# Weight-sum copies from SyncE between its loads, accumulations alone from GpSimd, and a sixth raw tile

## The chip, the core and the metric

The kernel runs on one core of a Trainium2 chip. Five engines work side by side, each in the order of its own instruction queue: TensorE (PE, matrix products, with its weight loads shown as PEld), VectorE (DVE), ScalarE (ACT), GpSimd (POOL) and SyncE (SP), which here only issues DMAs. GpSimd and ScalarE issue DMAs too. An engine that waits for a semaphore holds up everything behind it in its queue. The metric is the device time of one execution in microseconds (us); lower is better. The time before is the median of three runs, 763.82 us (761.96 to 764.92).

## What is computed

One layer of a streaming encoder on 512 frames of width 1024, all in float32:

```python
hn = rmsnorm(h, norm_mix_g[l])
proj = hn @ w_in[l]
fq, fk, fv, ff, gq, gf, gi, gg = jnp.split(proj, split_idx, axis=-1)
fox_out = fox_attention(...)         # 8 heads of 64, causal, with a forget bias F[t] - F[s]
rec = hgrn2_chunkwise(gq, gf, gi, lbs[l])   # 4 heads, state 128 x 128
h = h + jnp.concatenate([fox_out, rec], axis=-1) @ w_out[l]
mem_n = rmsnorm(mem, norm_mem_g[l])
h = h + memory_cross_attention(rmsnorm(h, norm_x_g[l]), mem_n, w_xq[l], w_xkv[l], w_xo[l])
u = rmsnorm(h, norm_ff_g[l]) @ w1[l]
h = h + jnp.square(jax.nn.relu(u)) @ w2[l]
return rmsnorm(h, final_norm_g)
```

w1 is 1024 x 4096 and w2 is 4096 x 1024. mem has 256 tokens.

## The kernel before, in words

**Precision.** Each float32 operand is split in two parts of a shorter type (hi and lo), and each product is the sum of three matmuls: hi by hi, hi by lo, lo by hi. For a weight this means: SyncE loads a raw half panel of 512 KB into a raw tile (names `wr...`), ScalarE writes its hi part (`wh...`, line 178), VectorE its lo part (`wl...`, line 182). The raw tile is free again when VectorE is done, and only then may SyncE issue the load that comes next into that tile. In the names a number is the panel and a or b its half: `wr19a` is the first half of panel 19. Up to the MLP there are two raw tiles (pool `wrp`) and four hi and four lo tiles.

**Stages.** TensorE runs in the order in which the program is written. It does the input projections (names gf, gq, gi, gg), the recurrence (lv, dg, pa, po, pst, with rec its normed output), the forgetting attention in 16 steps of 128 queries for a pair of heads (ps scores, pt transposed probabilities, pv output), the output projection (wo), the cross-attention (xq, xs, xo, xw) and the MLP. Between the steps of the recurrence and the attention a filler places matmuls of projections that are still to do (pq, pk, xv, xk), in doses counted in us. The other engines are put in order by the scheduler of the tile framework, with priorities; that order is fixed when the program is built.

**The attention's softmax.** For a step and head, GpSimd makes the bias (`bi`, lines 987 and 988) from a row of F that a DMA spreads over the partitions (`nF`, line 855, issued by ScalarE); VectorE adds it to the scores and takes the maximum (line 1007), ScalarE takes the exponential (line 1009), VectorE divides (lines 1010 and 1011), TensorE transposes (line 1019). mem is loaded by GpSimd (`mt`, line 861); ScalarE squares it for its norm (`m0j`, line 374).

**Weight sums.** In the MLP, six of eight groups of w1 and all eight of w2 use a product scheme with seven block products in place of eight. It needs sums of weight blocks, which are made in device memory while the earlier stages run. For each of 14 sets (`u` of w1, `d` of w2, with the group's number) there are four sums, called 5, 7, 6 and 4; each is a copy of a first operand (line 427) and an accumulating DMA that adds the second (line 425), 512 KB each. All 112 DMAs are issued by GpSimd. Their due times come from a ledger: each group of matmuls adds its nominal us (`Presum.tick`), and when the ledger passes the next due time, one DMA is emitted, with a wait for that matmul. `PACE` gives the gaps: every 4 us of the ledger from 25 on, none by the ledger from 106 on, every 3 from 183 and every 6 from 306. In the attention, where the ledger has its pause, one DMA is emitted at each of the 16 steps (`presum.emit()` in the loop over `pairs`). Two sets take turns.

```python
SUMS = {"5": ("00", "01"), "7": ("01", "11"), "6": ("5", "11"), "4": ("6", "10")}
```

**MLP loads.** There the raw tiles rotate over five places (`RAWS`), two of `wrp` and three of the pool `s4p`, and loads are issued up to seven ahead (`LOADS`).

## Time and profile before

| | before |
|---|---|
| median of 3 runs | 763.82 us (761.96 to 764.92) |
| profiled execution | 761.13 us |
| its span, first to last instruction | 759.4 us |
| TensorE busy | 747.1 us (98%) |
| VectorE, ScalarE, GpSimd busy | 533.4, 429.9, 227.0 us |
| granted TensorE clock | 0.999 |
| DMA moved | 162.86 MB, mean 214 GB/s |
| GpSimd's DMA queue (q0) | 64.52 MB, 38.9% of 16 engines' span |
| SyncE's DMA queue (q1) | 94.43 MB, 37.4% |
| ScalarE's DMA queue (q10) | 3.15 MB, 1.3% |

A row of a timeline gives start, length, engine, line, operation, output and inputs; in brackets stands the idle time of the engine before it and what ended it. A row of waits gives the sum, the number of times and the longest, in us. The chain of waits goes back from the last instruction, at each step to what released it. Of a DMA queue the view gives packets, MB and the share of the 16 DMA engines' time in the stretch asked for.

### The profile page before, as it was taken

The page shows a single profiled execution, that of the slowest core. Times are in us where ns is not written, and L with a number is a line of the kernel's source. Part 1 is how long each engine was busy: PE and PEld are TensorE (multiplying, and loading weights), DVE is VectorE, ACT ScalarE, POOL GpSimd, SP SyncE. Part 2 cuts the span into 40 slices and gives each one's busy share as a digit, 9 for nine tenths or more (in the row PEclk, how much of TensorE's full clock was granted, in tenths as well). Part 3 has the DMA queues.
Part 4 walks back from the last instruction along what each step waited for, and adds up shares of the span by engine and source line. Part 5 has one row for each costly group of instructions (what it writes and reads, how often), then busy time and mean ns, then how long its engine had stood idle before and what let it go on. Part 6 is the DMA issues. An engine that isn't in the chain of part 4 may idle for free.

```text
span 759.4 us, 12056 instructions
## 1 busy us (share of the span) xinstructions
PE 747.1 (98%) x4501; PEld 649.1 (85%) x4501; DVE 533.4 (70%) x844; ACT 429.9 (57%) x715; POOL 227.0 (30%) x322
## 2 busy tenths in 40 slices
PE   9999999999998999999999999999999999999996
PEld 6889888898887988888888888898989999998985
DVE  5647873676876755545555558888788787979697
ACT  5655564565664643335443476657575757574873
POOL 7218552353453426841112211111111110000014
PEclk9999999999999999999999999999999999999999
DMA  8676877676788799996679969898988998948342
GB/s 249 195 222 132 209 191 167 183 159 159 194 255 216 232 221 265 236 253 152 151 212 182 242 159 306 178 356 220 289 263 290 226 291 267 274 146 276 113 139 111
DMA packets 99580, 162.86 MB, mean 214 GB/s; under 512 B 6481, under 2 KB 67450, under 8 KB 99074
## 3 DMA queue, kind: packets, MB, share of 16 engines
q0 software_dynamic: 27968, 64.52, 38.9%
q1 hardware_dynamic: 69810, 94.43, 37.4%
q10 hardware_dynamic: 1744, 3.15, 1.3%
q8 instruction: 35, 0.57, 0.3%
q14 instruction: 23, 0.19, 0.1%
HBM read 157.87 MB, written 62.93 MB: 291 GB/s over the span
## 4 chain that ended last, share of the span: by engine, by line
PE 95%; DMA 2%; DVE 1%; ACT 1%; issue 1%; POOL 0%; ACTq 0%; SPq 0%
PE U L1504 4%; PE U L1503 4%; PE U L1505 4%; PE uU L1378 3%; PE uU L1377 3%; PE uU L1376 3%; PE xq L243 2%; PE wo L243 2%; PE xq L244 2%; PE xq L245 2%; PE xw L245 2%; PE xw L244 2%; PE xw L243 2%; PE u L245 2%; PE wo L244 2%; PE u L244 2%
## 5 line engine op out<-in xcount | busy, mean ns | idle before, releaser
L182 DVE TENSOR_TENSOR wld<-wrd,whd 128x1024 fp32r<-128x1024 f32 x56 | 68.5, 1225 | 19.4 <-ACT whd L178 19.4
L178 ACT ACTIVATE whd<-wrd 128x1024 fp32r<-128x1024 f32 x56 | 59.2, 1057 | 26.1 <-PE uV L1377 8.0
L425 POOL DMA_DIRECT2D wsd<-in_w_dram x32 | 34.7, 1084 | 104.0 <-PE uU L1378 22.1
L178 ACT ACTIVATE whu<-wru 128x1024 fp32r<-128x1024 f32 x42 | 44.4, 1057 | 36.5 <-PE uU L1377 16.6
L182 DVE TENSOR_TENSOR wlu<-wru,whu 128x1024 fp32r<-128x1024 f32 x42 | 50.5, 1228 | 12.8 <-ACT whu L178 12.8
L1503 PE MATMUL U<-whd,hb 128*128 128x512 f32 x120 | 46.8, 390 | 0.0
L1504 PE MATMUL U<-wld,hb 128*128 128x512 f32 x120 | 46.8, 390 | 0.0
L1505 PE MATMUL U<-whd,hb 128*128 128x512 f32 x120 | 46.7, 389 | 0.0
L425 POOL DMA_DIRECT2D wsu<-in_w_dram x24 | 28.5, 1186 | 53.9 <-PE xq L245 8.7
L987 POOL TENSOR_SCALAR bi<-nF,Ft 128x128 f32<-128x128 f32 (+3 forms) x32 | 22.5, 707 | 47.2 <-PE pt L1019 26.0
L1599 POOL TENSOR_TENSOR fa<-acc,gfin 128x512 f32<-128x512 f32 x4 | 6.5, 1654 | 86.2 <-DVE acc L1469 83.9
L427 POOL DMA_DIRECT2D wsd<-in_w_dram x16 | 10.9, 680 | 56.8 <-PE gq L245 14.5
L1378 PE MATMUL uU<-x_hi,wlu 128*128 128x256 f32 x96 | 27.2, 283 | 0.0
L1377 PE MATMUL uY<-xs_lo,whu 128*128 128x256 f32 x96 | 27.2, 283 | 0.0
L1378 PE MATMUL uU<-xs_hi,wlu 128*128 128x256 f32 x96 | 27.2, 283 | 0.0
L1376 PE MATMUL uY<-xs_hi,whu 128*128 128x256 f32 x96 | 27.2, 283 | 0.0
L1378 PE MATMUL uY<-xs_hi,wlu 128*128 128x256 f32 x96 | 27.2, 283 | 0.0
L1376 PE MATMUL uU<-xs_hi,whu 128*128 128x256 f32 x96 | 27.2, 283 | 0.0
L1377 PE MATMUL uU<-xs_lo,whu 128*128 128x256 f32 x96 | 27.2, 283 | 0.0
L1377 PE MATMUL uU<-x_lo,whu 128*128 128x256 f32 x96 | 27.2, 283 | 0.0
L1376 PE MATMUL uU<-x_hi,whu 128*128 128x256 f32 x96 | 27.1, 283 | 0.0
L1133 ACT ACTIVATE x_hi<-hT,gv 128x512 fp32r<-128x512 f32 x16 | 11.4, 715 | 27.5 <-DVE hT L1132 27.4
(996 smaller groups left out, 2679.4 us busy)
## 6 DMA issues: line engine op xcount, KB each, us to landing
wsd<-in_w_dram POOLq DMA_DIRECT2D x48, 512.0 KB, 6.5
wsu<-in_w_dram POOLq DMA_DIRECT2D x36, 512.0 KB, 6.7
wrd<-wsd SPq DMA_DIRECT2D x32, 512.0 KB, 5.2
wrd<-in_w_dram SPq DMA_DIRECT2D x24, 512.0 KB, 6.1
wru<-wsu SPq DMA_DIRECT2D x24, 512.0 KB, 4.8
wru<-in_w_dram SPq DMA_DIRECT2D x18, 512.0 KB, 5.9
wsd<-wsd POOLq DMA_DIRECT2D x16, 512.0 KB, 5.5
wsu<-wsu POOLq DMA_DIRECT2D x12, 512.0 KB, 5.1
```

Source lines behind the costliest of these rows:

```text
L178: ac.activation(hi, raw, AF.Copy)
L182: ve.tensor_tensor(lo, raw, f(hi), ALU.subtract)
L243: te.matmul(ps, wh, hi, start=n_ == 0 and not begun, stop=False)
L244: te.matmul(ps, wh, lo, start=False, stop=False)
L245: at = te.matmul(ps, wl, hi, start=False, stop=k == order[-1])
L425: yield gp.dma_start(dst, block(g, b), accum_op=ALU.add)
L1376: te.matmul(ps[:, i, :], whi[:, k, ws], xh[:, k, :], start=begin, stop=False, skip_group_check=True)
L1377: te.matmul(ps[:, i, :], whi[:, k, ws], xl[:, k, :], start=False, stop=False, skip_group_check=True)
L1378: at = te.matmul(ps[:, i, :], wlo[:, k, ws], xh[:, k, :], start=False, stop=k == UK - 1, skip_group_check=True)
L1503: te.matmul(ps, hi, whi[:, k, :], start=begin, stop=False, skip_group_check=True)
L1504: te.matmul(ps, hi, wlo[:, k, :], start=False, stop=False, skip_group_check=True)
L1505: at = te.matmul(ps, lo, whi[:, k, :], start=False, stop=k == 1, skip_group_check=True)
```

## The change

- The first operands of the sums are copied by SyncE. One copy is placed behind each half-panel load from panel 3 on, in a fixed order beside the loads. A copy waits for no tile. All 56 are listed at the start, those of two sets in turns.
- GpSimd issues only the 56 accumulations, at the times of the ledger; `PACE` has other gaps and its pause begins at 97. In the attention's loop nothing is emitted any more.
- The sums 6 and 4 swap their operands: the block of the weight is copied, the earlier sum is added to it. An accumulation whose source is a sum is cut into pieces of 2 KB.
- A tile `t4` (512 x 2 floats per partition) takes the place of the two tiles `t3`. The attention's scaled q and k share it (names `qs` and `ks` before, `qk` after), and it is a raw tile besides: for every third half panel from panel 22 on, and as one of six places in the MLP. `LOADS` is 8.
- The rows of F are issued by GpSimd instead of ScalarE.

```diff
-RAWS, HB, LOADS = 5, 4, 7
-PACE = (25.0, 4.0), (106.0, None), (183.0, 3.0), (306.0, 6.0)
+RAWS, HB, LOADS = 6, 4, 8
+COPIES = 3
+PACE = (25.0, 9.0), (97.0, None), (183.0, 4.6), (306.0, 9.5)
...
-    t3p = ctx.enter_context(tc.tile_pool(name="t3p", bufs=2))
+    t4p = ctx.enter_context(tc.tile_pool(name="t4p", bufs=1))
...
+    LATE = len(specs)
     for w in (w_out, w_xq, w_xo):
...
-        raw_ = wrp.tile([P, uk * nw], F32, tag="wr", name=f"wr{name}", padded_shape=[P, UK * UW])
+        state["halves"] += 1
+        if len(stream) >= LATE and state["halves"] % 3 == 0:
+            raw_ = t4(f"wr{name}")
+        else:
+            raw_ = wrp.tile([P, uk * nw], F32, tag="wr", name=f"wr{name}", padded_shape=[P, UK * UW])
...
+            if len(stream) >= COPIES and copies:
+                tc.keep_in_program_order(copies.popleft()())
             splits.append(split_of(hi[:, qs, :], lo[:, qs, :], raw_[:, qs, :]))
...
-    SUMS = {"5": ("00", "01"), "7": ("01", "11"), "6": ("5", "11"), "4": ("6", "10")}
+    SUMS = {"5": ("00", "01"), "7": ("01", "11"), "6": ("11", "5"), "4": ("10", "6")}
...
-        for name, add in (("5", 0), ("7", 0), ("5", 1), ("7", 1), ("6", 0), ("6", 1), ("4", 0), ("4", 1)):
-            dst, (a, b) = wsum[kind, g, name], SUMS[name]
-            if add:
-                yield gp.dma_start(dst, block(g, b), accum_op=ALU.add)
-            else:
-                yield gp.dma_start(dst, wsum[kind, g, a] if a in SUMS else block(g, a))
+
+        def first(name):
+            dma = nc.sync.dma_start(wsum[kind, g, name], block(g, SUMS[name][0]))
+            copied.add((kind, g, name))
+            return dma
+
+        def sums():
+            for name, (_, b) in SUMS.items():
+                while (kind, g, name) not in copied:
+                    copies.popleft()()
+                src = wsum[kind, g, b] if b in SUMS else block(g, b)
+                more = {"max_dma_last_dim": 2048} if b in SUMS else {}
+                yield gp.dma_start(wsum[kind, g, name], src, accum_op=ALU.add, **more)
+
+        return [lambda name=name: first(name) for name in SUMS], sums()
...
+    for i in range(0, len(sets), 2):
+        for some in zip(*(c for c, _ in sets[i : i + 2])):
+            copies.extend(some)
+    presum.jobs.extend(j for _, j in sets)
...
-            ac.dma_start(fF[h], Fd[h, :].partition_broadcast(P))
+            gp.dma_start(fF[h], Fd[h, :].partition_broadcast(P))
...
-            dma = presum.emit()
-            if dma is not None:
-                tc.keep_in_program_order(dma)
...
     def raw_tile(name):
         raw_n[0] += 1
+        if raw_n[0] % RAWS == 4:
+            return t4(f"wr{name}")
```

The order of instructions at three places. The names are the tiles written and read, with a running number; `wsd` and `wsu` are sums of w2 and w1 blocks, `in_w_dram` is w1 or w2.

GpSimd at the end of the recurrence's products (mov and F), before:

```order
L800 TENSOR_TENSOR mov_417<-mov_417,F_416 128x4x64
L802 TENSOR_TENSOR F_413<-F_413 128x8
L802 TENSOR_TENSOR F_416<-F_416 128x8
L425 DMA wsd_523<-in_w_dram 256x1x512
L425 DMA wsu_546<-in_w_dram 512x1x256
L861 DMA mt_1355<-in_mem_dram 128x1024
L427 DMA wsd_1385<-in_w_dram 256x1x512
L364 TENSOR_SCALAR m0re<-m0m 128x1
```

and after:

```order
L443 DMA wsd_196<-wsd_195 256x512
L763 DMA Fd<-Fr 8x512
L823 TENSOR_TENSOR mov_470<-mov_470,F_469 128x4x64
L823 TENSOR_TENSOR mov_473<-mov_473,F_472 128x4x64
L825 TENSOR_TENSOR F_469<-F_469 128x8
L825 TENSOR_TENSOR F_472<-F_472 128x8
L885 DMA mt_1409<-in_mem_dram 128x1024
L443 DMA wsu_200<-wsu_199 256x512
L373 TENSOR_SCALAR m0re<-m0m 128x1
```

The load of mem (mt) comes directly behind the last product; one accumulation stands ahead of the products and one behind the load.

SyncE in the last quarter of the attention, before:

```order
L198 DMA wr18a<-in_w_xkv_dram 128x4x256
L198 DMA wr18b<-in_w_xkv_dram 128x4x256
L198 DMA wr19a<-in_w_xkv_dram 128x4x256
L198 DMA wr19b<-in_w_xkv_dram 128x4x256
L198 DMA wr20a<-in_w_xkv_dram 128x4x256
L198 DMA wr20b<-in_w_xkv_dram 128x4x256
```

and after:

```order
L205 DMA wr18a<-in_w_xkv_dram 128x4x256
L433 DMA wsd_220<-in_w_dram 256x1x512
L205 DMA wr18b<-in_w_xkv_dram 128x4x256
L433 DMA wsu_224<-in_w_dram 512x1x256
L205 DMA wr22a<-in_w_out_dram 128x4x256
L205 DMA wr19a<-in_w_xkv_dram 128x4x256
L433 DMA wsd_225<-in_w_dram 256x1x512
L205 DMA wr19b<-in_w_xkv_dram 128x4x256
L433 DMA wsu_229<-in_w_dram 512x1x256
L205 DMA wr20a<-in_w_xkv_dram 128x4x256
```

A copy stands behind each load, and wr22a, the first half panel that goes into `t4`, has moved up ahead of wr19a.

VectorE at the same place, before (ISA is the sum of scores and bias with its maximum mx):

```order
L1007 ISA bi_2679,mx_2749<-ps_2746,bi_2679 128x512
L1007 ISA mx_2749 128x1
L182 TENSOR_TENSOR wl19a<-wr19a,wh19a 128x1024
L1007 ISA bi_2684,mx_2758<-ps_2755,bi_2684 128x512
L1007 ISA mx_2758 128x1
L1010 RECIPROCAL dn_2751<-dn_2751 128x1
```

and after:

```order
L1031 ISA bi_2722,mx_2793<-ps_2790,bi_2722 128x512
L1031 ISA mx_2793 128x1
L1031 ISA bi_2727,mx_2802<-ps_2799,bi_2727 128x512
L1031 ISA mx_2802 128x1
L185 TENSOR_TENSOR wl19a<-wr19a,wh19a 128x1024
L1034 RECIPROCAL dn_2795<-dn_2795 128x1
```

Both maxima are now taken ahead of wl19a, which waits for the load wr19a.

More of the change, by code (lines that the diff above doesn't have):

```diff
@@ L103, in q2, with t4 @@
         return q2p.tile([P, S], R, tag="q2", name=name)
-    def t3(name):
-        return t3p.tile([P, S], F32, tag="t3", name=name)
+    def t4(name):
+        return t4p.tile([P, D], F32, tag="t4", name=name)
     def t2(name, dt=F32, shape=(S,)):
@@ L165, in emit @@
     stream = []
-    state = {"used": 0}
+    state = {"used": 0, "halves": 0}
+    copies, copied = deque(), set()
     UW, UK = WT + FH, KC // 2
@@ L456, in emit @@
     presum = Presum()
+    sets = []
     for g in range(DFF // HG):
-        presum.jobs.append(sum_jobs("d", g))
+        sets.append(sum_jobs("d", g))
         if g + 2 in SEVEN:
-            presum.jobs.append(sum_jobs("u", g + 2))
+            sets.append(sum_jobs("u", g + 2))
+    for i in range(0, len(sets), 2):
+        for some in zip(*(c for c, _ in sets[i : i + 2])):
+            copies.extend(some)
+    presum.jobs.extend(j for _, j in sets)
     park = {}
@@ L811, in fox_proj @@
         fq[p] = [q2(f"q{p}{j}") for j in range(2)]
+        ts = t4(f"qk{p}")
         ps = mm(f"pq{p}")
         yield from gemm_fm(ps, wt, 0, hn_hi, hn_lo)
-        t = t3(f"qs{p}")
+        t = ts[:, 0:S]
         ve.scalar_tensor_tensor(t, ps, 0.125, rbc, op0=ALU.mult, op1=ALU.mult)
@@ L825, in fox_proj @@
         yield from gemm_fm(ps, wt, P, hn_hi, hn_lo)
-        t = t3(f"ks{p}")
+        t = ts[:, S:D]
         ve.tensor_tensor(t, ps, rbc, ALU.mult)
```

## The prediction

> **What bounds the kernel now.** I read the head of the page first, then TensorE's list of waits, then the busy time by stages, then the chain of waits around each idle stretch, and last the DMA view of the microseconds in which a late load was waiting.
>
> ```profile
> span 759.4 us, 12056 instructions
> PE 747.1 (98%) x4501; PEld 649.1 (85%) x4501; DVE 533.4 (70%) x844; ACT 429.9 (57%) x715; POOL 227.0 (30%) x322
> ...
> PE 95%; DMA 2%; DVE 1%; ACT 1%; issue 1%; POOL 0%; ACTq 0%; SPq 0%
> ```
>
> TensorE is the bound: 747.1 of 759.4 us busy, and 95% of the chain that ended last. Neither the copies nor the accumulations touch a matmul, so nothing can be won but TensorE's idle time, 12.3 us in all. Its waits, longest first:
>
> ```profile
> PE pt L1019 <- DVE dn L1010: 3.1, 1, 3.1
> PE pst L906 <- DVE rec L927: 1.5, 1, 1.5
> PE warm L355 <- DVE ones L359: 1.3, 1, 1.3
> ```
>
> The third is the start and cannot move; what is left of the 12.3 us is the end, behind the last matmul. So two waits stand open, one of 3.1 us and one of 1.5. By stages (span, then PE busy; the last columns are clock, DMA share and GB/s):
>
> ```profile
> 25.00:121.00 96.00, 96.00 (x699) 81.09 (x699) 61.98 (x115) 54.13 (x88) 46.20 (x61) 1.00 0.74 187
> 121.00:162.00 41.00, 39.37 (x231) 33.94 (x230) 22.85 (x47) 22.55 (x66) 16.55 (x30) 1.00 0.63 168
> 231.00:273.00 42.00, 38.95 (x324) 36.33 (x324) 28.00 (x66) 22.07 (x43) 14.31 (x23) 1.00 0.78 224
> 273.00:440.00 167.00, 167.00 (x833) 140.85 (x830) 92.90 (x139) 63.55 (x111) 60.89 (x62) 1.00 0.88 214
> 440.00:740.00 300.00, 300.00 (x1803) 269.17 (x1802) 242.77 (x293) 201.66 (x278) 31.86 (x38) 1.00 0.79 236
> ```
>
> From 273 to 740 us TensorE never waits: there the change can only lose. Both waits lie in the recurrence and the attention. The first, followed back (start, length, what):
>
> ```profile
> 118.07 0.63 POOL wsu L425
> 118.70 8.46 DMA mt<-in_mem_dram
> ...
> 130.67 1.04 ACT hj L923 x8
> ...
> 133.63 0.87 DVE rec L927 x3
> ...
> 134.64 1.13 PE pst L906 x8
> ```
>
> It begins with a weight-sum accumulation on GpSimd. The load of mem (mt) is queued behind it and lands at 127.16; ScalarE, which works in order, stands before its square (m0j), and everything behind that square, the norm of the recurrence (hj, hr, rec) among it, is late.
>
> The second:
>
> ```profile
> 229.92 1.13 DVE wl18a L182
> ...
> 231.12 8.23 DMA wr19a<-in_w_xkv_dram
> ...
> 239.37 1.07 ACT wh19a L178
> ...
> 243.50 1.22 PE pt L1019 x8
> ```
>
> A weight load of 512 KB takes 8.23 us, ScalarE waits for it with two exponentials of the softmax queued behind, and TensorE runs dry.
>
> **The change, part by part.** *The two GpSimd DMAs ahead of mem.* In the old order both stand between the last recurrence product (F) and the load of mem; in the new one that place is empty, the next accumulation comes behind the load.
>
> ```profile
> 113.64 0.22 POOL L802 TENSOR_TENSOR F<-F 128x8 f32<-128x8 f32 x1 [1.13 <-DVE mov L799]
> ...
> 118.07 1.18 POOL L425 DMA_DIRECT2D wsu<-in_w_dram  x1 [2.74 <-PE gi L273]
> 118.70 1.13 POOL L861 DMA_DIRECT2D mt<-in_mem_dram  x1
> ```
> ```profile
> 124.33 0.47 ACT L655 ACTIVATE fv<-gi,r 128x256 f32<-128x256 f32 x1
> 127.18 0.63 ACT L374 ACTIVATE m0j<-mt 128x512 f32<-128x512 f32 x1 [2.38 <-DMA mt<-in_mem_dram]
> ```
>
> So mem is issued at about 113.9 instead of 118.7, 4.8 us earlier; even if it took 8.46 us again it would land at 122.4, before ScalarE is free for it at 124.8. One accumulation, the one of the seventh tick, now stands a few rows earlier and may hold GpSimd 1 to 2 us longer; 2.4 us are to spare. ScalarE's wait of 2.38 goes, and rec with it is up to 2.38 earlier, more than the 1.49 us for which TensorE waited. Bounds: 0 (a slot of mem that is not free; the row above shows no wait) to -1.5. I take **-1.5**. Next to be late would be the POOL power (hr), 0.9 us behind.
>
> *The load wr19a.* What it stood against is seen in the DMA view of three short stretches: 227 to 230, when wr18b had been issued and waited; 247 to 249, when wr20b ran nearly alone; and 42 to 46, in which one first-operand copy ran.
>
> ```profile
> 226.42 0.37 SPq L198 DMA_DIRECT2D wr18b<-in_w_xkv_dram  x1
> 231.12 0.37 SPq L198 DMA_DIRECT2D wr19a<-in_w_xkv_dram  x1
> ...
> 245.86 0.37 SPq L198 DMA_DIRECT2D wr20b<-in_w_xkv_dram  x1
> ...
> 272.82 0.37 SPq L198 DMA_DIRECT2D wr24a<-in_w_out_dram  x1
> ```
> ```profile
> q0 software_dynamic: 231, 0.46, 97.6%
> q1 hardware_dynamic: 10, 0.01, 1.1%
> ```
> ```profile
> q1 hardware_dynamic: 516, 0.51, 76.0%
> ```
> ```profile
> q0 software_dynamic: 144, 0.52, 42.8%
> ```
>
> From 227 to 230 GpSimd's queue (q0) with one accumulation took 97.6% of the 16 engines and SyncE's (q1) 1.1%: an accumulation shuts the loads out. It costs 0.976 x 3 us for 0.46 MB, that is 3.3 us of all engines for 512 KB (0.52 MB). A load costs 0.76 x 2 = 1.5 us. A copy from GpSimd's queue costs 0.428 x 4 = 1.7 us. And a load that has the engines is quick: wr20b, issued at 245.86, was in by
>
> ```profile
> 249.34 1.06 ACT L178 ACTIVATE wh20b<-wr20b 128x1024 fp32r<-128x1024 f32 x1 [0.77 <-DMA wr20b<-in_w_xkv_dram]
> ```
>
> 3.5 us, of which 2.0 are not transfer (I put half ahead of it, half behind).
>
> In the new order no accumulation is left in the attention. Ahead of wr19a on SyncE's queue stand wr18b, one copy, and the load wr22a, which has gone up into the freed new tile. The price of a copy on SyncE's queue is not in the trace: no such copy ran there. Its ends are 1.5 us (a load of that size on that queue) and 3.3 us (an accumulation, the dearest transfer of that size); I take 1.7, the same bytes between the same tensors. Counted from 226.4 + 1.0: 1.5 (wr18b) + 1.7 + 1.5 (wr22a) + 1.5 (wr19a) = 233.6. The two rows of F (nF), moved from ScalarE's queue to GpSimd's, fall there too:
>
> ```profile
> q10 hardware_dynamic: 288, 0.52, 4.3%
> ```
>
> 4.3% of the 42 us from 231 to 273 is 1.8 us: 235.4, and 1.0 to be seen, 236.4 instead of 239.35. With a copy at 3.3 it is 238.0. From there to TensorE it was 4.13 us (239.37 to 243.50). In the new order VectorE does the second maximum before wl19a instead of after it, so the second exponential follows the first without waiting; by the rows that is 3.3 us. TensorE would go on at 239.7; it has work until
>
> ```profile
> 240.17 0.28 PE L245 MATMUL xk<-meh,wl18b 128*128 128x256 f32 x1
> 243.50 1.22 PE L1019 MATMUL pt<-ident,bi 128*128 128x128 f32 x8 [3.05 <-DVE dn L1010]
> ```
>
> 240.45. So the wait goes, with 0.7 us to spare; with a copy at 3.3 it is 0.9 us. I take **-3.05**, with bounds -3.05 and -2.2.
>
> *56 copies between the loads.* Each is one more issue of 0.37 us on SyncE (a row above), 21 us on an engine that mostly waits for tiles: nothing. On the DMA engines the copies are the same bytes as before in another queue. In the first stretch they delay loads by 1.7 to 3.3 us. The tightest load behind a copy that I found is wr3b:
>
> ```profile
> 41.43 1.23 DVE L182 TENSOR_TENSOR wl3b<-wr3b,wh3b 128x1024 fp32r<-128x1024 f32 x1 [1.35 <-ACT wh3b L178]
> ...
> 47.35 0.39 PE L243 MATMUL gq<-hn_hi,wh3b 128*128 128x512 f32 x1
> ```
>
> 4.7 us lie between the end of its split and its use: covered either way. The densest stretch is the end of the attention. From wr19a to wr24a, 41.7 us, SyncE issues 9 loads and 10 copies: 9 x 1.5 + 10 x 1.7 + 1.8 (nF) = 32.3 us of engine time. It fits at 1.7; at 3.3 it is 48.3, and 6.6 us are over. Bounds 0 to +6.6; I take 0.
>
> *The Trainium skill on this.* The page "DMA: Bandwidth & Descriptors", section "Issuing engines are not separate DMA queues", says that DMAs of the sync, scalar and gpsimd engines run on the same 16 engines and interleave, and that issuing from several saves only the sequencer's time. By it the copies would hinder the loads from SyncE's queue as they did from GpSimd's, and the second wait would mostly stay; that is the first rival. The trace agrees that the engines are shared, but the stretch from 227 to 230 shows no even interleaving.
>
> *GpSimd in the attention.* Sixteen sum DMAs, of 0.5 to 1.2 us of GpSimd each, give way to eight row loads; GpSimd is busy 14.31 of 42 us there. No cost. ScalarE loses eight issues. An hT load stands earlier; it waits for a slot on no wait that TensorE had.
>
> *From 273 on.* Accumulations come every 4.6 and 9.5 us of the ledger instead of a DMA every 3 and 6. Up to 440 that is 27 x 3.3 + 14 copies x 1.7 = 113 us of engine time against about 41 x 2.5 = 102: the DMA share there goes from 0.88 to about 0.95 (11 of 167 us). The loads alone stay far below it, and it is the sums that would be late, which the MLP reads only later. The sixth raw tile and LOADS 8 buy lead where TensorE does not wait. Nothing, bounds 0 to about +1 (ScalarE's and VectorE's order changes by a row or two there).
>
> **The sum.** Against the profiled execution, 761.13 us (span 759.4 and 1.7 around it): -1.49 - 3.05 = -4.54, that is 756.6. The median of the runs, 763.82, lies 2.7 above this execution; the same step from it gives **759.3 us**, 0.6% faster. About 0.5% (3.8 us) is what a measurement of this kernel tells from no change: below 760.0 is faster, above 767.6 slower.
>
> **The rivals.** *The loads stay as late.* wr19a is now last in one queue behind a copy and a load that were not there, and lands as before at 239.35. Then 239.37 + 3.3 = 242.7, 2.2 us of the second wait stay: -1.49 - 0.8 = -2.3, **761.5**. For it speaks that the bytes in those microseconds are about the same; against it, that the dear accumulations (3.3 us each) are gone from them. Chance 0.22.
>
> *SyncE's copies are dear.* In the rows above SyncE's queue moves 1 KB a packet (516 for 0.51 MB) where the copy from GpSimd's moves 3.6 KB (144 for 0.52 MB); a copy in small pieces may cost like an accumulation. At 3.3 us the end of the attention is 6.6 us over, with only two raw tiles as reserve: -1.49 - 2.15 + 6.6 = +3.0, **766.8**. Each 0.1 us more per copy adds 1.0, so from 3.4 it is slower by over 0.5%. For it: no row shows this price. Against: copies at 1.7 on the other queue. Chance 0.12.
>
> *A new wait.* The reordered ScalarE and VectorE rows, or the row loads of F behind GpSimd's work, make a wait of 1 to 3 us that takes part of the gain: about 761. Chance 0.10.
>
> **The numbers.** The forecast has 0.56. Its own range is 758.2 to 760.8 (the spread of the runs shown, and 0.7 us of either sign). With the rivals at 761 and 761.5 inside, the range is 757.8 to 765.5: it leaves out the dear copies and some tenths below. Faster: most of 0.56 and a little of the new wait, 0.52. Slower by over 0.5%: half of the dear copies and something for what I have not seen, 0.13. Within: 0.35.
>
> **What would show it.** TensorE's list of waits has neither pst behind rec nor pt behind dn over 1 us; mem lands before ScalarE is free; wr19a takes about 5 us; a DMA stretch of the attention with copies alone gives their price. I am wrong if ScalarE shows waits for wr loads of over 3 us between 150 and 275 with TensorE idle behind them, if the copies cost 3 us, or if TensorE waits at all after 273.

## The result, and the profile after

| | before | after |
|---|---|---|
| median | 764.97 us (761.96 to 769.67, 19 runs) | 761.73 us (759.85 to 765.83, 19 runs) |
| ratio to before | | 0.9959, 95% interval 0.9942 to 0.9977 |
| profiled execution | 761.13 us | 760.26 us |
| span | 759.4 us | 758.1 us |

The changed kernel is 0.41% faster, 3.1 us, with an interval of 1.8 to 4.4 us. By the bound set in the prediction that is within 0.5%, just. The two profiled executions lie only 0.87 us apart; why the medians lie further apart is found below, in a second execution of the kernel before and in the granted clocks of all runs.

First the head of the page of the changed kernel, then TensorE's list of waits:

```profile
span 758.1 us, 12049 instructions
...
PE 746.6 (98%) x4501; PEld 648.5 (86%) x4501; DVE 537.8 (71%) x844; ACT 430.1 (57%) x715; POOL 188.6 (25%) x274
```
```profile
PE pt L1043 <- DVE bi L1035: 1.8, 3, 0.9
PE warm L364 <- DVE ones L368: 1.3, 1, 1.3
PE gi L280 <- ACT gg L678: 1.2, 1, 1.2
PE dg L727 <- DVE z L694: 0.8, 1, 0.8
```

Both old waits are off the list. In their place stand five small ones (three of them in the row of pt). The table of stages (span, TensorE busy, and at the end clock, DMA share and GB/s) says where: TensorE gained 1.63 us between 121 and 162 and 1.90 between 231 and 273, and lost 2.03 between 25 and 121 and 0.69 between 162 and 231. From 273 to 740 it is busy throughout, as before.

```profile
25.00:121.00 96.00, 93.97 (x686) 79.19 (x685) 60.29 (x111) 51.67 (x83) 38.63 (x50) 1.00 0.87 230
121.00:162.00 41.00, 41.00 (x244) 35.76 (x243) 22.72 (x47) 23.44 (x69) 15.12 (x30) 1.00 0.54 156
162.00:231.00 69.00, 68.31 (x442) 58.80 (x441) 54.68 (x136) 46.21 (x98) 24.38 (x49) 1.00 0.67 216
231.00:273.00 42.00, 40.85 (x348) 38.11 (x347) 29.83 (x67) 23.47 (x46) 10.04 (x19) 1.00 0.94 306
```

The row of the kernel before from 162 to 231, which the prediction does not show:

```profile
162.00:231.00 69.00, 69.00 (x448) 59.65 (x447) 54.46 (x136) 45.65 (x98) 32.70 (x57) 1.00 0.79 203
```

**The two old waits.** The timelines of GpSimd and ScalarE around the load of mem:

```profile
115.68 0.63 POOL L885 DMA_DIRECT2D mt<-in_mem_dram  x1
```
```profile
126.54 0.63 ACT L383 ACTIVATE m0j<-mt 128x512 f32<-128x512 f32 x1
```

mem is issued straight behind the last F (115.53), and ScalarE comes to it without a wait (no bracket). The whole program runs 2.03 us later here, because of two of the new waits. Then the chain of waits around wr19a:

```profile
231.86 6.32 DMA wr19a<-in_w_xkv_dram
...
239.26 1.42 ACT bi L1033 x4
```

The load takes 6.32 us where it took 8.23, the two exponentials follow each other at once, and TensorE is back at 241.40 after a wait of 0.21 us, not 3.05.

**The new waits.** The four larger ones in TensorE's timeline (the fifth is the 0.21 us just told):

```profile
61.35 0.69 PE L727 MATMUL dg<-sta,mov 128*64 128x64 f32 x16 [0.85 <-DVE z L694]
99.74 0.50 PE L280 MATMUL gi<-wh7a,hn_hi 128*128 128x512 f32 x1 [1.18 <-ACT gg L678]
166.45 0.30 PE L1043 MATMUL pt<-ident,bi 128*128 128x128 f32 x1 [0.69 <-DVE bi L1035]
...
254.64 0.52 PE L1043 MATMUL pt<-ident,bi 128*128 128x128 f32 x3 [0.94 <-DVE bi L1035]
```

*dg at 61 and gi at 100.* In the old order the first accumulation was issued at 59.91; now one is issued at 40.32 and one at 49.84, beside SyncE's copies. The chain leads from dg to the load wr5b, whose tile comes free only when wl4b is done, and wr4b was late. In the DMA view of 42.5 to 45.5, while wr4b waited, GpSimd's queue (q0) with one accumulation had 91.2% of the engines, and a copy that SyncE had issued at 39.04 stood ahead of wr4b as well.

```profile
51.20 1.27 DVE wl4b L185
...
52.49 5.65 DMA wr5b<-in_w_in_dram
...
59.64 0.89 DVE wl5b L185
```
```profile
q0 software_dynamic: 220, 0.45, 91.2%
q1 hardware_dynamic: 100, 0.17, 15.6%
```

VectorE splits wl5b ahead of the small rows of the recurrence (Ac, z) for which dg waits. So wr5b is needed long before TensorE uses its panel.

*pt at 166.* No load is late there; a row of VectorE stands elsewhere. Before, VectorE scaled q (qs) and then the second half of mem (mt); now it is the other way round, and VectorE first waits 2.37 us for the norm of mem. The rows before, and after:

```profile
155.88 0.68 DVE L815 SCALAR_TENSOR_TENSOR qs<-pq,rbc 128x512 f32<-128x512 f32 x1
157.96 1.00 DVE L377 TENSOR_SCALAR mt<-mt,m1r 128x1024 f32<-128x1024 f32 x1 [1.41 <-POOL m1r L367]
```
```profile
157.39 1.09 DVE L386 TENSOR_SCALAR mt<-mt,m1r 128x1024 f32<-128x1024 f32 x1 [2.37 <-POOL m1r L376]
159.06 0.67 DVE L839 SCALAR_TENSOR_TENSOR qk<-pq,rbc 128x512 f32<-128x512 f32 x1
```

*pt at 254.* Behind wr20a SyncE issues two copies, not one, ahead of wr20b, and ScalarE then waits 2.86 us for that load:

```profile
240.96 1.21 SPq L433 DMA_DIRECT2D wsd<-in_w_dram  x2
244.17 0.38 SPq L205 DMA_DIRECT2D wr20b<-in_w_xkv_dram  x1
```
```profile
250.21 1.06 ACT L181 ACTIVATE wh20b<-wr20b 128x1024 fp32r<-128x1024 f32 x1 [2.86 <-DMA wr20b<-in_w_xkv_dram]
```

**The price of a copy.** Between 132 and 137 us SyncE's queue carried one load (wr11b) and one copy (wsu) and nothing else, 1.05 MB:

```profile
q1 hardware_dynamic: 1056, 1.05, 69.8%
```

0.698 x 5 = 3.5 us of all engines for both: 1.75 each, or 2.0 for the copy if the load costs the 1.5 that the prediction read. Not 3.3.

### The profile page after: what moved, and what is told of

It reads as the page before. It is cut to its first block, busy times and chain, and to the rows that moved or that the text cites. A ratio compares the mean times of both kernels' runs of the same rounds, so it can differ in the third digit from the quotient of the medians.

```text
span 758.1 us, 12049 instructions
## 1 busy us (share of the span) xinstructions
PE 746.6 (98%) x4501; PEld 648.5 (86%) x4501; DVE 537.8 (71%) x844; ACT 430.1 (57%) x715; POOL 188.6 (25%) x274
## 3 DMA queue, kind: packets, MB, share of 16 engines
q10 hardware_dynamic: 592, 1.05, 0.4%
## 4 chain that ended last, share of the span: by engine, by line
PE 83%; DVE 6%; ACT 4%; DMA 3%; issue 2%; POOL 1%; SPq 0%; ACTq 0%; DVEq 0%; POOLq 0%
PE U L1527 4%; PE U L1526 4%; PE U L1528 4%; PE uU L1401 3%; PE uU L1400 3%; PE uU L1399 3%; PE xq L252 2%; PE wo L252 2%; PE xq L253 2%; PE xq L254 2%; PE xw L252 2%; PE xw L254 2%; PE xw L253 2%; PE wo L253 2%; PE u L254 2%
## 5 line engine op out<-in xcount | busy, mean ns | idle before, releaser
L443 POOL DMA_DIRECT2D wsd<-in_w_dram x16 | 16.9, 1053 | 98.0 <-PE U L1528 18.6
L443 POOL DMA_DIRECT2D wsd<-wsd x16 | 14.3, 896 | 95.8 <-PE uU L1401 19.6
L1011 POOL TENSOR_SCALAR bi<-nF,Ft 128x128 f32<-128x128 f32 (+3 forms) x32 | 20.7, 654 | 60.5 <-PE pt L1043 32.8
L1622 POOL TENSOR_TENSOR fa<-acc,gfin 128x512 f32<-128x512 f32 x4 | 6.5, 1654 | 93.0 <-ACT hb L1475 91.2
L443 POOL DMA_DIRECT2D wsu<-in_w_dram x12 | 14.1, 1176 | 59.2 <-PE U L1528 20.3
```

Of the source, the lines that this page charges most:

```text
L443: yield gp.dma_start(wsum[kind, g, name], src, accum_op=ALU.add, **more)
```

## The experiments

The sum to explain: 4.33 us of old waits gone (1.49 and 2.84), 3.66 us of new ones come (0.85, 1.18, 0.69, 0.94). Ratios are to the kernel before, with 95% intervals.

| run | median, us | ratio |
|---|---|---|
| e1, accumulations of the recurrence later | 764.35 | 1.0000 (0.9978 to 1.0022) |
| e2, copies later | 759.86 | 0.9946 (0.9925 to 0.9967) |
| e3, no copies in the attention's tail | 760.40 | 0.9946 (0.9926 to 0.9967) |
| e4, the mt row where it was | 760.71 | 0.9951 (0.9926 to 0.9977) |
| e5, these joined | 760.85 | 0.9944 (0.9924 to 0.9964) |
| e6, before with an earlier pause | 764.82 | 1.0011 (0.9997 to 1.0026) |
| e7, accumulations back in the attention | 772.73 | 1.0111 (1.0094 to 1.0129) |
| e8, without the tile t4 | 767.76 | 1.0050 (1.0031 to 1.0069) |
| e10, before with mem first | 765.20 | 1.0013 (0.9995 to 1.0031) |
| e11, joined, rows of F on ScalarE | 759.23 | 0.9932 (0.9918 to 0.9946) |
| e12, rows of F on ScalarE | 760.43 | 0.9955 (0.9944 to 0.9967) |

The intervals of e2 to e5, e11 and e12 all overlap that of the changed kernel (0.9942 to 0.9977). What each of these edits takes away is therefore read from its trace, which is one execution, and not from its median. The times of a run are medians of 5 to 12 executions.

### Accumulations of the recurrence later

```diff
-PACE = (25.0, 9.0), (97.0, None), (183.0, 4.6), (306.0, 9.5)
+PACE = (97.0, None), (183.0, 4.0), (306.0, 8.5)
...
-            self.jobs, self.spent, self.next, self.at = deque(), 0.0, PACE[0][0], None
+            self.jobs, self.spent, self.next, self.at = deque(), 0.0, 183.0, None
```

> The changed kernel, but no accumulation before the pause of the ledger ends: the nine of the recurrence come later (every 4.0 and 8.5 us of the ledger in place of 4.6 and 9.5). The copies stay where they are. Theory (accumulations in the recurrence): TensorE's two new waits there (dg behind z, 0.85 us; gi behind gg, 1.18 us) go, wr4b lands some 3.3 us earlier than 50.1, and the kernel takes about 2.0 us less than the changed one, 0.6 to 0.7% less than the kernel before. Rival (the copies behind the loads make both waits): wr5b and with it dg stay as late, at least 1.5 of the 2.0 us stay, and the time is that of the changed kernel within 0.5 us.

Measured, by TensorE's waits and by two stages:

```profile
PE xs L1212 <- ACT xqh L1196: 1.1, 1, 1.1
PE xs L1214 <- DVE xql L1197: 0.9, 1, 0.9
```
```profile
25.00:121.00 96.00, 96.00 (x700) 81.10 (x700) 61.51 (x116) 54.15 (x88) 34.00 (x45) 1.00 0.65 198
273.00:440.00 167.00, 164.98 (x796) 138.60 (x796) 93.95 (x136) 62.16 (x109) 55.53 (x51) 0.99 0.96 219
```

dg and gi no longer wait, with every copy in its place: from 25 to 121 TensorE is busy throughout. The rival does not hold in this trace. But the total is that of the kernel before. Of the accumulations that came later, four more run between 273 and 440 (31, where the changed kernel has 27) and four more behind 440. Between 273 and 440 stand two new waits of 2.03 us, the waits at 240 and 254 are 0.84 and 1.50 us here, and after the new waits the granted clock drops (below). The accumulations can't simply be pushed back.

### Copies later

```diff
-COPIES = 3
+COPIES = 10
...
-                    copies.popleft()()
+                    tc.keep_in_program_order(copies.popleft()())
```

> The changed kernel, but copies stand behind every load only from panel 10 on; before that only those that an accumulation needs at once are issued (eight fewer between wr3b and wr10a). All other engines keep their order to the row. Theory: the wait of dg (0.85 us) goes, because one copy (1.5 us of the engines) fewer stands before wr4b and 0.85 is less than 1.5; the wait of gi (1.18 us) stays over 0.8 us, because it comes from VectorE's order (lf before sta) and not from a load. Total about 0.8 us less than the changed kernel. Rival (copies make both waits): both go, 2.0 us less.

dg does not wait, and gi does not either; a wait of 0.22 us behind z is left in this stage. So my explanation of gi by VectorE's order falls: the order is the same to the row and the wait is gone. gi waits because the recurrence is late since wr5b. With the run before this: taking away the accumulations, or all copies but those that an accumulation needs, was each enough in its trace. For the copies that is not so in every execution. In e11 (below) as few copies stand there, and the order of SyncE, GpSimd, ScalarE and VectorE is the one of e2 up to 110 us; but wr5b took 5.96 us, where e2 had it within 5.2, and dg waits 0.45 us and gi 1.17 again. How much the copies add to what the accumulations do is open.

Two waits of the changed kernel are still there: 0.69 us at 165, and 1.24 us at 253 in place of 0.94. Part of the gain hides behind a wait of 0.5 us at the start (gf behind wh0a) that only this execution has.

### No copies in the attention's tail

```diff
-            if len(stream) >= COPIES and copies:
+            if len(stream) >= COPIES and not 18 <= len(stream) <= 22 and copies:
```

> The changed kernel without copies behind the loads of panels 18 to 22; they follow later, one behind each load. Theory (copies ahead of loads on the same queue, 1.5 us each): wr19a lands 1 to 1.5 us earlier than 238.2, ScalarE's wait for wr20b (2.86 us) falls under 1 us, TensorE's waits of 0.21 and 0.94 us behind bi go, total 1.1 us less than the changed kernel. Rival (the rows of F and hT on GpSimd's queue hold the loads up, or the engines are shared evenly whatever the queue): wr19a stays at 238 within 0.5 us and the wait of 0.94 stays over 0.6.

The wait at 254 is gone, that at 241 is 0.22 us. ScalarE's rows:

```profile
237.45 1.06 ACT L181 ACTIVATE wh19a<-wr19a 128x1024 fp32r<-128x1024 f32 x1 [1.98 <-DMA wr19a<-in_w_xkv_dram]
...
247.45 1.06 ACT L181 ACTIVATE wh20b<-wr20b 128x1024 fp32r<-128x1024 f32 x1 [0.80 <-DMA wr20b<-in_w_xkv_dram]
```

For wr20b the theory holds (0.80 us of wait, not 2.86). For wr19a it was too high: 0.75 us earlier, not 1 to 1.5. The copies that went to the stretch from 273 to 440 (22, where the changed kernel has 12) raise its DMA share to 0.99, and TensorE does not wait there, while in e1, with four accumulations more and 12 copies, it waited at a share of 0.96. So the share alone does not decide; that accumulations weigh more fits, but was not tried by itself.

### The mt row where it was

The scaling of mem's second half is called later and made to depend on the scaling of q:

```diff
-        ve.scalar_tensor_tensor(t, ps, 0.125, rbc, op0=ALU.mult, op1=ALU.mult)
+        state["q"] = ve.scalar_tensor_tensor(t, ps, 0.125, rbc, op0=ALU.mult, op1=ALU.mult)
...
+    nosync = mybir.DependencyInfo(mybir.DependencyClass.Sync, mybir.DependencyReason.DATA)
+    tc.add_manual_dep(mt_late.pop()().ins, state["q"].ins.name, nosync, reason="mt")
```

> The changed kernel with one row of VectorE moved: the scaling of the second half of mem (mt, behind m1r) stands two rows later, where it stood in the kernel before, behind mx_lo and the scaling of q. All else is in the same order. Theory: ScalarE's q follows at about 156.5 in place of 159.8, wh12a at about 158.4 in place of 161.7, and TensorE's wait of 0.69 us at 166 goes; total 0.7 us less than the changed kernel. Rival (the tile that q and k now share makes q late, whatever the order): q stays at 159 to 160 and the wait stays.

```profile
159.09 1.05 ACT L181 ACTIVATE wh12a<-wr12a 128x1024 fp32r<-128x1024 f32 x1
```

q follows at 157.19, wh12a at 159.09 where it was 161.66, and the wait at 166 is gone, wholly: one row of VectorE made it. The total does not show it (0.9951 against 0.9959): in this execution the waits at dg and at 255 are 1.08 and 1.46 us, 0.23 and 0.52 longer than in the changed kernel's. When the planner moves the row is seen in e6, e8 and e10 below: the row moves too, and 0.69 us are waited, where q and k have their own tiles, and in the kernel before as soon as GpSimd has fewer DMAs at the end of the recurrence. It looks as if the scheduler then reckons with an earlier norm of mem than GpSimd delivers; its reckoning is not on record.

### These joined

The edits of e2 and e4, and another number of copies behind a load:

```diff
-            if len(stream) >= COPIES and copies:
+            n_copies = 0 if len(stream) < COPIES or 18 <= len(stream) <= 21 else 2 if 11 <= len(stream) <= 14 else 1
+            for _ in range(min(n_copies, len(copies))):
                 tc.keep_in_program_order(copies.popleft()())
```

> The changed kernel with three things put together: few copies before panel 10 (as in the run of the late copies), none behind the loads of panels 18 to 21, and the row of mt two places later on VectorE; for it two copies, not one, behind each load of panels 11 to 14, where the DMA engines were 43 to 57% busy. Theory: all five new waits of TensorE (3.87 us together) go, at most 0.5 us of them stays; span about 755, time 1.9 us under the run of the late copies, 0.8% under the kernel before. Rival (work that was pushed back waits elsewhere: the copies behind panels 11 to 14 hold up the loads of the attention's first half, or the sums come late from 273 on): a new wait of over 1 us between 150 and 440, and the time is that of the run of the late copies or more.

```profile
PE pt L1048 <- DVE bi L1040: 1.4, 1, 1.4
```

It has the shortest span of all, 755.2 us, and 757.36 us in the profiled execution, but one wait of 1.42 us, at 239.5, was not foreseen, and the median is not apart from that of the changed kernel. So four of the five waits go, as in the theory, and the fifth grows to over 1 us, as in the rival. wr19a took 7.5 us. From 229 to 233, while GpSimd's queue carried the two rows of F, the queues together kept the engines only three quarters busy, though wr19a was waiting:

```profile
q0 software_dynamic: 144, 0.49, 54.9%
q1 hardware_dynamic: 167, 0.28, 20.0%
```

### Accumulations back in the attention

```diff
                 fox_biases(n + 1)
+            dma = presum.emit()
+            if dma is not None:
+                tc.keep_in_program_order(dma)
```

> The changed kernel with one thing put back: GpSimd emits one accumulation at each of the attention's 16 steps, beside SyncE's copies (fewer are left for later). Theory (an accumulation costs the engines 3.3 us and shuts out SyncE's loads): wr19a takes over 8 us again, TensorE's waits behind bi or dn between 162 and 273 grow by 3 us or more from 1.84, and the total is 2 us or more above the changed kernel. Rival (queues share the engines evenly, as the page DMA: Bandwidth & Descriptors of the Trainium skill says in Issuing engines are not separate DMA queues; the second wait went through the order of the maxima alone): the waits grow by less than 1 us.

```profile
234.87 10.73 DMA wr19a<-in_w_xkv_dram
```
```profile
PE pt L1043 <- DVE bi L1035: 7.9, 4, 5.6
```

The strongest result: 11 us above the changed kernel. wr19a takes 10.73 us and TensorE stands still for 5.57 us at once. That accumulations are gone from the attention is what shortened the second wait; the order of the two maxima alone does not.

### Without the tile t4

q and k have the two tiles `t3` again, and no half panel goes into `t4`:

```diff
-RAWS, HB, LOADS = 6, 4, 8
+RAWS, HB, LOADS = 5, 4, 7
...
-        t = ts[:, 0:S]
+        t = t3(f"qs{p}")
...
-        if raw_n[0] % RAWS == 4:
-            return t4(f"wr{name}")
```

> The changed kernel without the tile t4: q and k have their two small tiles again, the raw tiles are two up to the MLP and five there, LOADS is 7. By this wr22a stands behind wr21b again, and VectorE splits wl19a ahead of the second maximum, as in the kernel before. Theory (the tile gave the attention nothing but the order of the maxima, and its load is one more ahead of wr19a): wr19a lands about 1.5 us earlier than 238.2, the chain from it to TensorE is 0.8 us longer, so the wait at 241 stays under 0.5; the wait of 0.69 at 166 stays, since the mt row stands where it stood; the MLP is unchanged within 0.3 us. Total within 0.7 us of the changed kernel. Rival (the tile is what removed the second wait): pt waits over 1.5 us at 241 to 244.

```profile
PE xq L252 <- ACT x_hi L1153: 2.1, 1, 2.1
...
PE pt L1042 <- DVE dn L1033: 0.9, 1, 0.9
PE xq L253 <- DVE x_lo L1154: 0.8, 1, 0.8
```
```profile
312.79 11.06 DMA wr27b<-in_w_xq_dram
```

In the attention it is between the two: 0.94 us behind dn at 244, more than the 0.5 I allowed, less than the rival's 1.5. wr19a took 6.12 us, so having no wr22a ahead of it saved 0.2 us, not 1.5. What neither foresaw is 2.9 us in the cross-attention, where wr27b takes 11.06 us and only two raw tiles stand against it. So the third tile from panel 22 on seems to be what keeps the copies and accumulations of that stretch off TensorE, by this one trace. (That dg waits 2.0 us here can hardly come from the tile, which is not a raw tile there yet: the order up to there is that of the changed kernel, and the wait is 0.8 to 1.1 us in the five other traces with the same copies and accumulations. So the same order can cost 0.8 to 2.0 us.)

### Before with an earlier pause, and with mem first

```diff
-PACE = (25.0, 4.0), (106.0, None), (183.0, 3.0), (306.0, 6.0)
+PACE = (25.0, 4.0), (97.0, None), (183.0, 3.0), (306.0, 6.0)
```

> The kernel before with one edit: the pause of the ledger begins at 97 in place of 106, so that the load of mem stands directly behind the last product F on GpSimd, ahead of the two accumulations. In the attention all is issued as before, though each DMA is one or two places further back in the list. VectorE's mt row moves ahead of mx_lo and q's scaling in this order too. Theory (two separate waits): pst behind rec (1.49 us) goes, pt behind dn stays at 2 us or more, a wait of 0.7 us behind bi appears at about 165; total 0.8 us less than the kernel before. Rival (the first wait also gave the second its place, so that the time saved is waited for later): pt behind dn grows by about 1.5 us and the total stays.

This edit did not do what its text says: the two accumulations ahead of mem were due at 81 and 85 of the ledger and stayed. mem was issued at 118.33 and pst waited its 1.49 us. It shows two things all the same. With two DMAs fewer later on GpSimd, the mt row moved and pt waited 0.69 us at 166. And the second wait, which the theory put at 2 us or more, was 0.96 us, although all weight sums of the attention still stood there: the list has slipped, and at 230.45 GpSimd issues a copy where the kernel before issues an accumulation at 229.35.

```profile
232.16 6.07 DMA wr19a<-in_w_xkv_dram
```

This points to the accumulation just ahead of that load as what made it long, not to the number of DMAs in the attention. With the pause from 80 on:

```diff
-PACE = (25.0, 4.0), (106.0, None), (183.0, 3.0), (306.0, 6.0)
+PACE = (25.0, 4.0), (80.0, None), (183.0, 3.0), (306.0, 6.0)
```

> The kernel before with the pause of the ledger from 80 on: five DMAs fewer in the recurrence, and the load of mem stands directly behind the last product F on GpSimd (in the run before it two accumulations still stood ahead). Theory: mem is issued at about 113.9, ScalarE waits for it under 0.2 us, pst behind rec (1.49 us) goes or falls under 0.3. The wait of 0.7 us behind bi at about 165 comes, since VectorE's mt row stands two places earlier; the second wait, with other DMAs in the attention's 16 steps, may be anything from 1 to 3 us. Rival (mem is not what rec waits for; it is hr on GpSimd or ScalarE's row of work): mem lands early and pst waits over 1 us all the same.

```profile
113.92 0.63 POOL L861 DMA_DIRECT2D mt<-in_mem_dram  x1
```
```profile
124.74 0.63 ACT L374 ACTIVATE m0j<-mt 128x512 f32<-128x512 f32 x1
```

mem is issued at 113.92, ScalarE does not wait, pst is off the list: the first wait did hang on the two accumulations ahead of mem. And yet the median does not move. pt waits 0.69 us at 164 (the mt row) and 1.86 at 241, where wr19a took 6.99 us behind a copy. And 4.2 us of waits stand after 273: 2.2 up to 440, where as many DMAs of GpSimd run as before (41), and 2.0 behind it, where seven more run. What makes them is not shown; e6 has 1.9 us of waits up to 440 with 41 DMAs too. A wait that is removed by moving work is only won if the work costs nothing where it goes.

### Rows of F on ScalarE

```diff
-            gp.dma_start(fF[h], Fd[h, :].partition_broadcast(P))
+            ac.dma_start(fF[h], Fd[h, :].partition_broadcast(P))
```

In the joined kernel:

> The joined kernel with the rows of F issued by ScalarE again, as in the kernel before. Theory (while the row loads of GpSimd's queue run, SyncE's queue nearly stands still, 229 to 233 us in the joined kernel): wr19a takes at most 5.5 us in place of 7.5, TensorE's wait of 1.42 us behind bi falls under 0.4, span about 754. Rival (the bytes of the rows hold the loads up on any queue): wr19a stays over 7 us and the wait over 1 us.

and in the changed kernel:

> The changed kernel with only the rows of F issued by ScalarE again. VectorE's and ScalarE's orders change by a few rows with it. Theory: wr19a lands 1 to 2 us earlier against its issue than in the changed kernel (6.3 us), and the total falls by at most 0.5 us, since only 0.21 us of TensorE's waits hang on it. Rival (the eight issues on ScalarE cost what the change saved there): ScalarE's work before 273 is later by over 1 us and the total rises by 0.5 us or more.

In the joined kernel wr19a takes 7.52 us again (7.54 before) and pt waits 1.40 us: the rival's signs are there, and the queue from which the rows come makes no difference. That the rows are what makes this load long is likely by the DMA view, but no run leaves them out, and in e3 the load took 5.40 us beside them. From 231 to 235 the engines were again only 77% busy with a load waiting (q10 is ScalarE's queue):

```profile
q1 hardware_dynamic: 434, 0.62, 48.6%
q10 hardware_dynamic: 227, 0.42, 28.5%
```

In the changed kernel wr19a takes 6.1 us, 0.2 less, and the total is the same within the intervals, so neither queue is shown to be worth anything. In this trace, though, the wait at 241 is gone and that at 254 is 0.22 us, with both copies ahead of wr20b; with the rows on GpSimd and the same copies it was 0.94, 1.50, 1.24 and 1.46 (the changed kernel, e1, e2, e4). One trace does not tell whether the rows did that. The joined kernel with the rows on ScalarE has the lowest median of all, 759.23 us, though its profiled execution (760.51) still shows dg, gi and pt waiting (0.45, 1.17 and 1.40 us) and xs 0.73 us at 332. Its interval and that of the changed kernel just overlap, so that it is faster than before is shown, and that it is faster than the changed kernel is likely but not shown.

### The kernel before, once more

> The kernel before, unchanged, in a second profiled execution. Its median is 3 us above the execution that the prediction read, that of the changed kernel 1.5 us. Theory (the first trace was a lucky one): this one shows the same two waits (pst behind rec 1.5, pt behind dn about 3) and 1 to 3 us of further waits that the first does not have, most of them behind loads or behind the engines that split them; span 761 to 763. Rival (the difference is not in waits, but in the clock or in what lies around the span): the same two waits and no others over 0.5 us.

```profile
PE 748.7 (98%) x4501; PEld 650.2 (85%) x4501; DVE 534.8 (70%) x844; ACT 430.1 (56%) x715; POOL 227.4 (30%) x322
```
```profile
PE pt L1019 <- DVE dn L1010: 3.4, 1, 3.4
...
PE U L1503 <- DVE acc L1471: 0.7, 2, 0.5
```

763.70 us, 2.6 above the first profiled execution and 3.4 above the changed kernel's, which is what the medians say. Only 1.0 us of the 2.6 are waits (0.7 of them in the MLP); TensorE itself is 1.6 us longer busy, with the same 4501 matmuls. The table of stages in steps of 4 us finds the place. Column before the last two: the granted clock. First the second execution of the kernel before, then the first one:

```profile
244.00:248.00 4.00, 4.00 (x23) 4.00 (x22) 3.10 (x11) 1.63 (x7) 2.75 (x5) 0.57 0.41 129
```
```profile
244.00:248.00 4.00, 4.00 (x36) 3.94 (x35) 3.46 (x11) 2.32 (x7) 3.01 (x5) 1.00 0.32 104
```

Behind the wait of 3.38 us the clock was 0.57 for 4 us, 0.43 x 4 = 1.7 us lost; behind the wait of 3.05 in the first execution it was 1.00. The theory (more waits) explains 1.0 us, its rival (the clock) 1.6. The prediction read an execution in which the wait cost only its own length.

## Why the prediction was right, and where it was not

**Which case came.** The forecast named both old waits as the gain, and both went. The time came out 2.4 us above the 759.3 forecast, in the range, faster than before but not by 0.5%. The rival that describes it best is "a new wait" (about 761, chance 0.10): the measured median is 761.73. It should have had more.

That the time came out so near is in part luck. The sum left out 3.66 us of new waits, and it left out what else the long wait cost in most executions of the kernel before ("The sum", below). The two errors have opposite signs. With the first alone, the step from 763.82 would have ended near 763, outside the forecast's own 758.2 to 760.8, though inside the whole range.

**Term 1, mem, -1.49: right.** mem was issued at 113.92 in e10 (forecast about 113.9), and ScalarE stood before it at 124.74 without waiting (forecast 124.8). What I left out is that VectorE's order changes with it, 0.69 us.

**Term 2, wr19a, -3.05: right in its mechanism, measured -2.84.** I had the load land at 236.4, 4.1 us before TensorE runs out of work at 240.45. In e2 ScalarE took it at 236.44, but that agreement is chance: the first wait is gone there, all runs earlier, and TensorE's work ends at 239.66, 3.2 us behind the load. In the changed kernel the two are 238.20 and 241.19, 3.0 us apart. So the load came about 1 us later than forecast, which used up the reserve of 0.7 us; it took 6.3 us, not about 5. From the load to TensorE it was 3.2 us in both (forecast 3.3). e7 shows that accumulations lengthen this load, and e6 points to the one just ahead of it. The price of a copy, the unknown of this term, was 1.7 in the forecast and is 1.75 to 2.0.

**"56 copies between the loads": wrong, and this step cost the forecast most.** It called the loads of the first stretch covered, by 4.7 us at wr3b, measured from the end of the split to the panel's use on TensorE. But a split holds up what stands behind it on VectorE, and for wr5b that is z, for which TensorE waits at once: 0.85 us, and 1.18 more at gi. That the first accumulations come 20 us earlier than before (40.32 against 59.91) was not costed at all. In e1, without these accumulations, the waits are away; with few copies they are away in e2 and e5 and in part there in e11. So the accumulations look needed, by one trace, and the share of the copies is open.

**The end of the attention, 0: missed by 0.94 us** (0.22 to 1.50 in the five traces with the same copies there). The sum of engine time fits, as computed; but the sum says nothing of one load with two copies in front of it. e3, without them, has no such wait.

**"ScalarE's and VectorE's order changes by a row or two": priced at nothing, measured 0.69 us.** e4 shows it. One row is enough if what it waits for comes from another engine.

**From 273 on, 0: right, for a reason that I denied.** I wrote that the sixth raw tile buys lead where TensorE does not wait. In the one trace without the tile it waits 2.9 us (e8).

**The rivals.** "The loads stay as late" with its rule from the Trainium skill (page "DMA: Bandwidth & Descriptors", section "Issuing engines are not separate DMA queues") did not happen: the load came 1.9 us sooner after its issue. The trace agrees with the Trainium skill for the rows of F: from either queue the load beside them took the same time (7.54 and 7.52 us). The section does not fit the accumulations: e7's 10.73 us against 6.32 are no even interleaving. (It says that DMAs interleave; the "evenly" of e7 goes beyond its words.) "SyncE's copies are dear" fell with their price.

**The sum.** -4.33 + 3.66 = -0.67 in waits, -0.87 between the two profiled executions. The medians differ by 3.2. The second execution of the kernel before says why: 763.70 - 760.26 = 3.44, of which 1.7 are clock and 1.7 waits.

The mean granted clock of every run bears out the clock's part. Of the 14 profiled executions, the five with a drop while TensorE works have 0.993 to 0.996, the nine without one 0.997 to 0.999. The kernel before ran 68 more times beside the experiments: 54 times at 0.996 or less, and once at 0.999, as in the execution that the prediction read. Of the changed kernel's 19 executions four had 0.996 or less, and these are the four longest (764.39 to 765.83 us). The means are 0.9953 and 0.9974; 0.0021 of 762 us is 1.6 us, an estimate, since the drop at the very end, behind the last matmul, is in these means too. It is half of the 3.2. The other half is the 0.67 of waits above and about 1 us more of waits, as the second execution has them; for that part there is this one trace. What made the clock drop in those four executions of the changed kernel is not on record.

## What to carry to other kernels

The slack of a load ends where the first instruction behind its split has to run, not where its panel is used; look at the queue of the splitting engine before a transfer is put ahead of a load. Moving DMA work removes a wait only if it is priced again at the place where it goes, and a planner's order is to be compared to the row after each such move. Before a stall is priced by one trace, compare the granted clock of that execution with those of the other runs, and take a second trace: the same stall can cost its length, or its length and a drop of the clock.

## What the runs showed of the hardware

**A wait of about 2 us or more can lower TensorE's clock for some 4 us.** Beside the second execution of the kernel before, it is seen in e1 behind two waits of 1.15 and 0.88 us, 1.4 us apart, in e10 behind 1.86 (0.79 and 0.78 in two steps of 4 us), in e8 behind 2.08 and 0.81, and in e7 behind 5.57 (0.50 and 0.71). The rows of e1:

```profile
332.00:336.00 4.00, 2.43 (x12) 2.04 (x13) 2.52 (x3) 0.64 (x2) 0.00 (x0) 0.86 1.10 250
336.00:340.00 4.00, 4.00 (x20) 3.52 (x19) 1.37 (x5) 1.20 (x4) 0.00 (x0) 0.71 1.09 294
```

(0.14 + 0.29) x 4 = 1.7 us are lost. In e10 and e8 it is 1.7 each, in e7 2.7 of the time for which TensorE was busy (0.50 x 3.17 + 0.29 x 4). Behind the first trace's 3.05 us and a 2.01 in e8 it did not come, and behind no wait of 1.5 us or less that stood alone. The Trainium skill, page "TensorE: Matmul & The Clock Gate", section "What's actually happening", tells of a window of about 3.4 us that runs freely, after which an idle array gets half its clock until a busy window has passed; half of 3.4 is 1.7, an estimate from that figure, which agrees with the 1.7 us seen here; and a free window fits that equal waits differ. That waits of about 2 us are enough is not what it says; there the measurement decides.

**An accumulating DMA crowds out plain loads, a copy of the same size delays them far less.** 16 accumulations in the attention made wr19a 10.73 us long; with copies alone around it, it took 6.32, and without them 5.40 (e3). In the kernel before, an accumulation just ahead of it gave 8.23 and 8.57, a copy in its place 6.07 and 6.99 (e6, e10).

**While a row is spread over 128 partitions, loads can slow down and engines idle.** In e5 and e11 they were 75 and 77% busy with a load waiting, on GpSimd's queue as on ScalarE's. It is not always so: in the changed kernel from 234 to 236 the rows' queue had 65.9%, SyncE's 35.2%, together all of the engines. Why is open.

**Waits in the MLP (U behind acc or V, 0.7 to 2.0 us) stand in three of four traces with all weight sums on GpSimd, and in none of ten with copies on SyncE.** They stay away without the tile t4 too (e8), so it is not the tile; what makes them was not tried.
